# Logsumexp over heads on one core: new sharing of the heads between engines in the last fifteen tiles, and 1 MB half tiles for the last seven instead of two

## The chip, the cores and the metric

The kernel runs on one core of a Trainium2 chip. The metric is the device time in microseconds (us) of one execution. The profile's span, from the first to the last instruction, is about 2 us shorter than that time (335.9 us for 338.01 in the profiled run of the kernel before, 332.8 for 334.57 after the change). Five kinds of engine do the work in these kernels: PE (matrix products), ACT (one function on each element), DVE (products and sums of vectors), POOL (here mainly the adds of the bias) and the DMA engines, which move data; the SP queue issues the loads and most of the output. The tiles lie in SBUF; PE writes to PSUM, a second memory from which ACT and DVE read here (L165 and L193 of the kernel before).

## The reference

```
x: (8, 2048, 2048) f32, bias: (8, 256) f32       # 8 heads of 256 columns
x_heads = x.reshape(B, S, H, Dh).transpose(0, 2, 1, 3) + bias[None, :, None, :]
x_tiled = np.repeat(x_heads, 2, axis=2)          # each row twice
out     = max + log(sum(exp(x_tiled - max)))     # over the 256 columns of a head
```

So 134 MB are read once, and for every row and head one number is written twice. Inputs are random normal, so the kernels leave the maximum out. The sum needs either exp(x + b), or exp(x) times the weight exp(b).

## The kernel before

The input is cut into 64 tiles of 2 MB (128 partitions x 2 rows x 2048 columns), nine of them in SBUF at once. In a tile the eight heads are treated in three ways:

- PE heads (2): PE adds the bias while it copies the columns to PSUM (a 3-row matmul of the bias, then a matmul by the identity); ACT takes the exponential and sums it in one instruction for each head and row.
- POOL heads (4): POOL adds the bias in SBUF, ACT takes the exponential, DVE sums.
- DVE heads (2): ACT takes the exponential without the bias, DVE multiplies by the weights exp(b) and sums.

The steady part does tile t's adds, then the exponentials and sums of tile t - 1. "Bulk" below means this.

```
def exp_and_sum(t):                              # for tile t, called one tile later
    v = xts[t % NBUF][:, :, CPE:D]               # 6 heads: 4 with POOL's bias, 2 without
    exp_inplace(v)                               # ACT, L202
    f = v[:, :, CG:CW]
    nc.vector.tensor_tensor(out=f, in0=f, in1=w_tile, op=ALU.mult)     # DVE, L193
    nc.vector.tensor_reduce(out=R[b][:, :, NPE:H, blk], ...)           # DVE, L194
...
for t in range(T):
    if left >= NLATE:                            # all but the last two tiles
        got = add_bias([xt[:, k, 0:CPE] for k in range(K)])            # PE, L154, L159
        g_add(t)                                                       # POOL, L186
    if 0 < t and left >= NLATE - 1:
        exp_and_sum(t - 1)
    if left >= NLATE:
        for k in range(K): sum_biased(got[k], ...)                     # ACT, L165
    for k0, k1, c0, c1 in pieces(t) if left < NLATE else []:           # last two tiles
        ...  exp_inplace(...); sum_biased(...)
        weigh(...)       # DVE, L208: multiply by the weights and sum, one head and row each
    if 0 < t and t - 1 + NBUF < T: load(t - 1 + NBUF)                  # SP queue
```

The last two tiles (62 and 63) are "prompt": no POOL, each piece done as it comes, six heads by DVE's weighted sums. They are loaded as halves (1 MB, one of the two rows) and, at the very end, smaller pieces. At the end of each batch of 8 tiles, `finish` transposes the sums on PE (L224), takes the logarithm on ACT (L237), and sends it out by DMA.

The softmax here doesn't subtract the row's maximum and nothing guards it: scores larger than these inputs give would overflow.

## Time and profile before

| | before |
|---|---|
| time, median of 4 runs | 337.78 us (337.74 to 337.91) |
| span of the profiled run | 335.9 us |
| landing of a 2 MB tile | every 4.9 us |
| last piece of input landed (landing records of the trace) | 322.1 us |

These are lines of the page of the kernel before: busy us of each engine with its share of the span, then busy tenths in 40 slices of 8.4 us, the busy share of the DMA engines and the GB/s.

```profile
span 335.9 us, 2193 instructions
PE 236.6 (70%) x410; PEld 69.5 (21%) x410; DVE 290.2 (86%) x174; ACT 296.1 (88%) x598; POOL 291.6 (87%) x84
...
DVE  0019999999999999989989999988999999979995
ACT  1379999899999999999899999998999889899994
DMA  7999999999999999999999999999999999999900
GB/s 296 430 427 435 429 424 427 433 423 427 428 425 430 433 423 430 425 428 431 424 433 421 429 427 425 434 432 423 425 430 427 433 427 426 427 429 418 386 23 16
```

The DMA row is full from the second slice to the 38th: the loads bound the run until about 322 us. From the second slice to the 36th the rate is 421 to 435 GB/s; whether the loads themselves could be made faster was not tested. Three engines are at 86 to 88%, yet none of them sets the pace there: on the page POOL waits 23.8 us in all for loaded tiles, ACT 9.8 us for POOL, and DVE 34.1 us for ACT (22.7 of them before its first tile). In the last two slices the DMA is idle and ACT and DVE still work: that is the part that can be shortened. The next lines are groups of instructions, from the page: line, engine, operation, tiles, shapes and count, then busy us and the mean ns of one, then idle time just before.

```profile
L186 POOL TENSOR_TENSOR xt<-xt,b_rep 128x2048 f32<-128x2048 f32 x62 | 281.2, 4537 | 26.2 <-DMA xt<-in_x_dram 23.8
L194 DVE TENSOR_REDUCE R<-xt 128x12 f32<-128x3072 f32 x62 | 208.0, 3355 | 7.2 <-DVE xt L193 1.0
L193 DVE TENSOR_TENSOR xt<-xt,w_rep 128x1024 f32<-128x1024 f32 x62 | 75.5, 1218 | 34.3 <-ACT xt L202 34.1
L208 DVE CUSTOM_DVE_ANT_0 junk<-xt,w_rep 128x256 f32<-128x256 f32 x24 | 8.3, 416 | 0.0
```

A bulk tile goes through POOL (4.54 us), ACT (2.76 us) and DVE (1.22 + 3.36 us) one after the other. Each fits into 4.9 us, but one tile needs the sum of them. The timeline of the kernel before shows what this means at the end (start us, duration us, engine, line, operation; in brackets the idle time before it and what ended it):

```profile
312.17 4.54 POOL L186 TENSOR_TENSOR xt<-xt,b_rep 128x2048 f32<-128x2048 f32 x1 [0.35 <-DMA xt<-in_x_dram]
...
316.74 4.14 ACT L202 ACTIVATE xt<-xt 128x3072 f32<-128x3072 f32 x2 [0.34 <-POOL xt L186]
...
319.54 1.22 DVE L193 TENSOR_TENSOR xt<-xt,w_rep 128x1024 f32<-128x1024 f32 x1 [0.22 <-ACT xt L202]
324.13 0.41 DVE L208 CUSTOM_DVE_ANT_0 junk<-xt,w_rep 128x256 f32<-128x256 f32 x1
```

Tile 61, the last bulk tile, landed at 312.0 and left DVE at 324.2, 12.2 us later. Only then could DVE begin with the prompt sums of tile 62, although its first half had landed at 314.5. From the chain of work that ended last in the kernel before (start us, duration us, what):

```profile
327.97 0.33 DVE junk L208
...
332.07 0.33 DVE junk L208
332.46 0.39 PE tpair L224
332.88 0.37 ACT res L237
```

The run ends with a row of DVE's weighted sums, 24 in all at one every 0.342 us (324.13 to 332.41), then a transpose, a logarithm and 2.6 us of output.

### The profile page before, as it was taken

How to read it: one execution, taken by the hardware profiler on the slowest of the kernel's cores; microseconds unless marked ns; L12 is line 12 of the kernel's file. 1: busy time of each engine (PE TensorE's matmuls, PEld its weight loads, DVE VectorE, ACT ScalarE, POOL GpSimd, SP SyncE). 2: the span in 40 equal slices, each digit the busy share in tenths (PEclk: the TensorE clock that was granted, in tenths of full speed). 3: DMA queues.
4: the chain of work that ended last, by engine and by line, in shares of the span. 5: the costliest groups of instructions: out<-in, count | busy, mean ns of one | idle time of the engine just before them, and what ended most of it. 6: DMA issues, size and time to landing. Idle time of an engine off the chain costs nothing. (4 is left out here: it accounts for less than half of the span.)

```text
span 335.9 us, 2193 instructions
## 1 busy us (share of the span) xinstructions
PE 236.6 (70%) x410; PEld 69.5 (21%) x410; DVE 290.2 (86%) x174; ACT 296.1 (88%) x598; POOL 291.6 (87%) x84
## 2 busy tenths in 40 slices
PE   5297687796766866677577669867668695767761
PEld 2022221222121221122122112212112221212110
DVE  0019999999999999989989999988999999979995
ACT  1379999899999999999899999998999889899994
POOL 6999989979989999899898999898998999889613
PEclk9998965559789589876987775676987659587875
DMA  7999999999999999999999999999999999999900
GB/s 296 430 427 435 429 424 427 433 423 427 428 425 430 433 423 430 425 428 431 424 433 421 429 427 425 434 432 423 425 430 427 433 427 426 427 429 418 386 23 16
DMA packets 11199, 135.41 MB, mean 403 GB/s; under 512 B 1577, under 2 KB 1849, under 8 KB 2993
## 3 DMA queue, kind: packets, MB, share of 16 engines
q1 hardware_dynamic: 10832, 135.17, 95.1%
q0 software_dynamic: 352, 0.10, 0.2%
q8 instruction: 3, 0.05, 0.1%
q14 instruction: 10, 0.08, 0.1%
q10 hardware_dynamic: 2, 0.01, 0.0%
HBM read 134.23 MB, written 1.05 MB: 403 GB/s over the span
## 5 line engine op out<-in xcount | busy, mean ns | idle before, releaser
L186 POOL TENSOR_TENSOR xt<-xt,b_rep 128x2048 f32<-128x2048 f32 x62 | 281.2, 4537 | 26.2 <-DMA xt<-in_x_dram 23.8
L159 PE MATMUL ps<-xt,ident 128*128 128x512 f32 x256 | 183.5, 855 | 66.2 <-DMA xt<-in_x_dram 65.7
L194 DVE TENSOR_REDUCE R<-xt 128x12 f32<-128x3072 f32 x62 | 208.0, 3355 | 7.2 <-DVE xt L193 1.0
L202 ACT ACTIVATE xt<-xt 128x3072 f32<-128x3072 f32 (+3 forms) x70 | 177.5, 2539 | 10.2 <-POOL xt L186 9.8
L165 ACT ACTIVATE ps<-ps 128x256 f32<-128x256 f32 x256 | 94.6, 369 | 17.2 <-PE ps L159 12.7
L193 DVE TENSOR_TENSOR xt<-xt,w_rep 128x1024 f32<-128x1024 f32 x62 | 75.5, 1218 | 34.3 <-ACT xt L202 34.1
L159 PEld LDWEIGHTS ps<-xt,ident 128*128 128x128 f32 x256 | 57.5, 249 | 153.9 <-DMA xt<-in_x_dram 98.5
L154 PE MATMUL ps<-b,ones 3*128 3x512 bf16 x128 | 48.0, 450 | 12.6 <-DMA b<-bparts 6.5
L165 ACT ACTIVATION_READ_ACCUMULATOR ps<-ps 128x1 f32 x256 | 48.8, 191 | 0.0
L154 PEld LDWEIGHTS <-ones 3*128 3x128 bf16 x128 | 7.8, 97 | 78.2 <-issue 78.2
L258 POOL DMA_DIRECT2D out_dram<-res x8 | 4.0, 508 | 9.5 <-ACT res L237 9.5
L224 PE MATMUL tpair<-ident,R 128*64 128x128 f32 (+1 forms) x16 | 4.3, 367 | 10.0 <-DVE R L194 10.0
L208 DVE CUSTOM_DVE_ANT_0 junk<-xt,w_rep 128x256 f32<-128x256 f32 x24 | 8.3, 416 | 0.0
L132 PE MATMUL w_rep<-brow,ones 1*128 1x512 f32 x6 | 5.5, 1078 | 3.4 <-DMA brow<-in_bias_dram 3.4
L237 ACT ACTIVATE res<-tpair 64x512 f32<-64x512 f32 (+3 forms) x11 | 6.0, 543 | 2.0 <-PE tpair L224 2.0
L139 ACT ACTIVATE b_rep<-w_rep 128x1024 f32<-128x1024 f32 x1 | 1.0, 1025 | 6.9 <-PE w_rep L132 6.9
L224 PEld LDWEIGHTS tpair<-ident,R 128*64 128x64 f32 (+1 forms) x16 | 1.9, 143 | 19.2 <-DVE R L194 16.4
L224 PE MATMUL tpair<-ident,Rz 128*8 128x128 f32 x2 | 0.7, 372 | 3.4 <-ACT xt L202 1.8
L132 PEld LDWEIGHTS w_rep<-brow,ones 1*128 1x128 f32 x6 | 1.8, 325 | 5.4 <-issue 5.4
L121 POOL CAST bparts<-brow 1x512 bf16<-1x512 f32 x1 | 0.6, 601 | 2.0 <-DMA brow<-in_bias_dram 2.0
L105 ACT ACT_TABLE_LOAD x1 | 1.3, 1283 | 0.7 <-PEq L344 0.7
L142 ACT ACTIVATE w_rep<-w_rep 128x512 f32<-128x512 f32 x3 | 1.7, 582 | 0.1
(18 smaller groups left out, 9.5 us busy)
## 6 DMA issues: line engine op xcount, KB each, us to landing
xt<-in_x_dram SPq DMA_DIRECT2D x62, 2048.0 KB, 32.0
xt<-in_x_dram SPq DMA_DIRECT2D x2, 1024.0 KB, 30.0
xt<-in_x_dram SPq DMA_DIRECT2D x2, 512.0 KB
out_dram<-res SPq DMA_DIRECT2D x7, 128.0 KB, 30.1
xt<-in_x_dram SPq DMA_DIRECT2D x3, 256.0 KB, 16.4
xt<-in_x_dram SPq DMA_DIRECT2D x2, 128.0 KB, 8.7
out_dram<-res POOLq DMA_DIRECT2D x8, 12.0 KB, 1.7
b<-bparts POOLq DMA_DIRECT2D x3, 1.0 KB, 5.7
```

What stands on the lines that cost most here:

```text
L132: nc.tensor.matmul(w_rep[:, c : c + MM], lhsT=ones, rhs=brow[:, CPE + c : CPE + c + MM], start=True, stop=True,)
L154: nc.tensor.matmul(p[:, 0:CPE], lhsT=ones3, rhs=b3, start=True, stop=False)
L159: nc.tensor.matmul(p[:, 0:CPE], lhsT=ident, rhs=v, start=False, stop=True)
L165: nc.scalar.activation(out=p[:, c : c + Dh], in_=p[:, c : c + Dh], func=ACT.Exp, accum_out=dst(h),)
L186: nc.gpsimd.tensor_tensor(out=v, in0=v, in1=b_tile, op=ALU.add)
L193: nc.vector.tensor_tensor(out=f, in0=f, in1=w_tile, op=ALU.mult)
L194: nc.vector.tensor_reduce(out=R[b][:, :, NPE:H, blk], in_=v.rearrange("p k (h j) -> p k h j", j=Dh), op=ALU.add, axis=mybir.AxisListType.X,)
L202: nc.scalar.activation(out=v, in_=v, func=ACT.Exp)
L208: nc.vector.tensor_tensor_reduce(out=j, in0=v, in1=w_rep[:, c : c + Dh], scale=1.0, scalar=0.0, op0=ALU.mult, op1=ALU.add, accum_out=dst,)
L224: nc.tensor.transpose(out=tps[i][0:nr, k], in_=src(k), identity=ident)
L237: nc.scalar.activation(out=rv, in_=tv, func=ACT.Ln)
L258: engine.dma_start(out=ov, in_=iv)
```

## The change

The intent is to have less work left when the last data land. Tiles 0 to 48 stay bulk (other columns go to each engine, the amounts are the same). From tile 49 a "mixed" stage: PE takes one head, POOL three, and DVE weighs the other four at once, without waiting for POOL. From tile 57 tiles are loaded and worked on as two halves. From tile 61 all is prompt. Weights used beside POOL's adds are in PSUM (`w_ps`); those of the heads that only the prompt stage weighs are in SBUF (`w_sb`).

```
-NPE = 2
-CG = 1024
-NLATE = 2
+BULK = dict(pe=2, g0=4, late=True)      # pe: PE heads; g0: first POOL head; late: DVE heads wait
+MIXED = dict(pe=1, g0=5, late=False)
+PROMPT = dict(pe=2, g0=8, late=False)
+STAGES = [(0, BULK, False), (49, MIXED, False), (57, MIXED, True), (61, PROMPT, True)]
-LAST_CUTS = [[0, 1024, 2048], [0, 512, 1024, 1536, 1792, 2048]]
+LAST_CUTS = [[0, 2048], [0, 1024, 1536, 2048]]
... (ps: five buffers for four; w_ps, w_sb; add_bias, g_add and exp_and_sum take a stage and rows)
+        for k0, k1, c0, c1 in pieces(t):
+            if c0 == 0:
+                got = add_bias(m, ...)                          # PE
+                if with_pool: g_add(m, xt, k0, k1)              # POOL
+            if waiting: waiting()        # the piece before: exponential and sums of its POOL heads
+            if h0 < h1 and not m["late"]: exp_inplace(...)      # ACT, at once
+            if c0 == 0: ... sum_biased(m, ...)                  # ACT
+            if not m["late"]: ... weigh(...)                    # DVE, at once
+            waiting = next_waiting                              # also issues the load of tile t + 9
```

More of the change, by code (lines that the diff above doesn't have):

```diff
@@ L43 @@
     T = B * NBLK
-    CPE = NPE * Dh
-    CW = D - CPE
+    CPE = 2 * Dh
     MM = 512
-    assert CPE <= MM
+    W0, G0, W1 = Dh, 4 * Dh, 5 * Dh
     sb = ctx.enter_context(tc.tile_pool(name="sb", bufs=1))
@@ L54 @@
     brow = sb.tile([1, D], F32, name="brow")
-    b_rep = sb.tile([P, CG], F32, name="b_rep")
+    b_rep = sb.tile([P, D - G0], F32, name="b_rep")
+    w_sb = sb.tile([P, D - W1], F32, name="w_sb")
     ident = sb.tile([P, P], F32, name="ident")
@@ L69, with mode_of, halves_of @@
     xts = [sb.tile([P, K, D], F32, name=f"xt{i}") for i in range(NBUF)]
-    w_rep = pp.tile([P, CW], F32, name="w_rep")
-    ps = [pp.tile([P, MM], F32, name=f"ps{i}") for i in range(4)]
+    w_ps = pp.tile([P, W1 - W0], F32, name="w_ps")
+    ps = [pp.tile([P, MM], F32, name=f"ps{i}") for i in range(5)]
     tpair = pp.tile([P, 2, K, P], F32, name="tpair")
     tps = [tpair[:, i] for i in range(2)]
+    def mode_of(t):
+        return [m for t0, m, _ in STAGES if t0 <= t][-1]
+    def halves_of(t):
+        return [s for t0, _, s in STAGES if t0 <= t][-1]
     def pieces(t):
-        left = T - 1 - t
-        if left > 1:
+        if not halves_of(t):
             return [(0, K, 0, D)]
-        cuts = [[0, D]] * K if left else LAST_CUTS
+        cuts = [[0, D]] * K if t < T - 1 else LAST_CUTS
         return [
@@ L127, with spread, add_bias @@
         nc.gpsimd.dma_start(out=b3[i : i + 1, :], in_=bparts[:, i])
-    for c in range(0, CW, MM):
+    def spread(dst, c0, c1):
         nc.tensor.matmul(
-            w_rep[:, c : c + MM],
-            lhsT=ones,
-            rhs=brow[:, CPE + c : CPE + c + MM],
-            start=True,
-            stop=True,
-        )
-    nc.scalar.activation(out=b_rep, in_=w_rep[:, 0 : CG], func=ACT.Copy)
-    for c in range(0, CW, MM):
-        w = w_rep[:, c : c + MM]
+            dst, lhsT=ones, rhs=brow[:, c0:c1], start=True, stop=True
+        )
+    for i, c in enumerate(range(G0, D, MM)):
+        spread(ps[i], c, c + MM)
+        nc.scalar.activation(
+            out=b_rep[:, c - G0 : c - G0 + MM], in_=ps[i], func=ACT.Copy
+        )
+    for c in range(W0, W1, MM):
+        w = w_ps[:, c - W0 : c - W0 + MM]
+        spread(w, c, c + MM)
         nc.scalar.activation(out=w, in_=w, func=ACT.Exp)
+    nc.scalar.activation(out=w_sb, in_=b_rep[:, W1 - G0 :], func=ACT.Exp)
     n_ps = [0]
     n_junk = [0]
-    def add_bias(views):
+    def add_bias(m, views):
+        n = m["pe"] * Dh
         got = []
@@ L154, in add_bias @@
             nc.tensor.matmul(
-                p[:, 0:CPE], lhsT=ones3, rhs=b3, start=True, stop=False
+                p[:, 0:n], lhsT=ones3, rhs=b3[:, 0:n], start=True, stop=False
             )
@@ L158, in add_bias, with sum_biased @@
         for p, v in zip(got, views):
-            nc.tensor.matmul(p[:, 0:CPE], lhsT=ident, rhs=v, start=False, stop=True)
+            nc.tensor.matmul(p[:, 0:n], lhsT=ident, rhs=v, start=False, stop=True)
         return got
-    def sum_biased(p, dst):
-        for h in range(NPE):
+    def sum_biased(m, p, dst):
+        for h in range(m["pe"]):
             c = h * Dh
@@ L170, in sum_biased, with each_row, g_add, exp_inplace @@
             )
-    b_tile = bass.AP(
-        tensor=b_rep.tensor,
-        offset=b_rep.offset,
-        ap=[b_rep.ap[0], [0, K], [1, CG]],
-    )
-    w_tile = bass.AP(
-        tensor=w_rep.tensor,
-        offset=w_rep.offset + CG,
-        ap=[w_rep.ap[0], [0, K], [1, CW - CG]],
-    )
-    def g_add(t):
-        v = xts[t % NBUF][:, :, CPE : CPE + CG]
-        nc.gpsimd.tensor_tensor(out=v, in0=v, in1=b_tile, op=ALU.add)
-    def exp_and_sum(t):
-        b, blk = divmod(t, NBLK)
-        v = xts[t % NBUF][:, :, CPE:D]
-        exp_inplace(v)
-        f = v[:, :, CG:CW]
-        nc.vector.tensor_tensor(out=f, in0=f, in1=w_tile, op=ALU.mult)
+    def each_row(src, c, n, k_rows):
+        return bass.AP(
+            tensor=src.tensor,
+            offset=src.offset + c,
+            ap=[src.ap[0], [0, k_rows], [1, n]],
+        )
+    def g_add(m, xt, k0, k1):
+        c = m["g0"] * Dh
+        v = xt[:, k0:k1, c:D]
+        nc.gpsimd.tensor_tensor(
+            out=v, in0=v, in1=each_row(b_rep, c - G0, D - c, k1 - k0), op=ALU.add
+        )
+    def exp_inplace(v):
+        nc.scalar.activation(out=v, in_=v, func=ACT.Exp)
+    def later(m, xt, k0, k1, sums):
+        h0 = m["pe"] if m["late"] else m["g0"]
+        v = xt[:, k0:k1, h0 * Dh : D]
+        exp_inplace(v)
+        if m["late"]:
+            n = (m["g0"] - h0) * Dh
+            f = v[:, :, 0:n]
+            nc.vector.tensor_tensor(
+                out=f,
+                in0=f,
+                in1=each_row(w_ps, h0 * Dh - W0, n, k1 - k0),
+                op=ALU.mult,
+            )
         nc.vector.tensor_reduce(
-            out=R[b][:, :, NPE:H, blk],
+            out=sums[:, k0:k1, h0:H],
             in_=v.rearrange("p k (h j) -> p k h j", j=Dh),
@@ L199, in exp_and_sum @@
         )
-    def exp_inplace(v):
-        nc.scalar.activation(out=v, in_=v, func=ACT.Exp)
     def weigh(v, h, dst):
-        c = h * Dh - CPE
+        c = h * Dh
+        w = w_ps[:, c - W0 : c - W0 + Dh] if c < W1 else w_sb[:, c - W1 : c - W1 + Dh]
         j = junk[n_junk[0] % 2]
@@ L210, in weigh @@
             in0=v,
-            in1=w_rep[:, c : c + Dh],
+            in1=w,
             scale=1.0,
@@ L272, in finish_batch, with sums_of @@
         )
+    def sums_of(t):
+        b, blk = divmod(t, NBLK)
+        if t < T - 2:
+            return R[b][:, :, :, blk]
+        return Ry if t < T - 1 else Rz
+    waiting = None
     for t in range(T):
-        b, blk = divmod(t, NBLK)
+        m = mode_of(t)
         xt = xts[t % NBUF]
-        left = T - 1 - t
-        def sum_at(k, h):
-            if left > 1:
-                return R[b][:, k, h, blk : blk + 1]
-            return (Ry if left else Rz)[:, k, h : h + 1]
-        if left >= NLATE:
-            got = add_bias([xt[:, k, 0:CPE] for k in range(K)])
-            g_add(t)
-        if 0 < t and left >= NLATE - 1:
-            exp_and_sum(t - 1)
-        if left >= NLATE:
-            for k in range(K):
-                sum_biased(got[k], lambda h: sum_at(k, h))
-        for k0, k1, c0, c1 in pieces(t) if left < NLATE else []:
-            if left == 0 and c1 == D and k0 > 0:
+        sums = sums_of(t)
+        with_pool = m["g0"] < H
+        for k0, k1, c0, c1 in pieces(t):
+            if t == T - 1 and c1 == D and k0 > 0:
                 finish(
@@ L305, with next_waiting @@
             if c0 == 0:
-                got = add_bias([xt[:, k, 0:CPE] for k in range(k0, k1)])
-            w0 = max(c0, CPE)
-            if w0 < c1:
-                exp_inplace(xt[:, k0:k1, w0:c1])
+                got = add_bias(m, [xt[:, k, 0 : m["pe"] * Dh] for k in range(k0, k1)])
+                if with_pool:
+                    g_add(m, xt, k0, k1)
+            if waiting:
+                waiting()
+            h0 = max(c0 // Dh, m["pe"])
+            h1 = min(c1 // Dh, m["g0"])
+            if h0 < h1 and not m["late"]:
+                exp_inplace(xt[:, k0:k1, h0 * Dh : h1 * Dh])
             if c0 == 0:
                 for k in range(k0, k1):
-                    sum_biased(got[k - k0], lambda h: sum_at(k, h))
-            for k in range(k0, k1):
-                for c in range(w0, c1, Dh):
-                    weigh(xt[:, k, c : c + Dh], c // Dh, sum_at(k, c // Dh))
-            if left == 0 and c0 == 0:
+                    sum_biased(m, got[k - k0], lambda h: sums[:, k, h : h + 1])
+            if not m["late"]:
+                for k in range(k0, k1):
+                    for h in range(h0, h1):
+                        weigh(
+                            xt[:, k, h * Dh : (h + 1) * Dh], h, sums[:, k, h : h + 1]
+                        )
+            def next_waiting(t=t, m=m, xt=xt, k0=k0, k1=k1, sums=sums):
+                if m["g0"] < H:
+                    later(m, xt, k0, k1, sums)
+                if k1 == K and t + NBUF < T:
+                    load(t + NBUF)
+            waiting = next_waiting
+            if t == T - 1 and c0 == 0:
                 if k0 == 0:
@@ L320 @@
                     finish(B - 1, lambda k: Ry[:, k], 1, K, S - 2 * K * P, 0, nc.sync)
-        if 0 < t and t - 1 + NBUF < T:
-            load(t - 1 + NBUF)
         fb, at = divmod(t - 2, NBLK)
```

## The prediction

> **What bounds the kernel now.** The loads. The page's slices show the DMA at 9 tenths and about 428 GB/s from slice 2 to slice 36; the waits show PE (65.7 us) and POOL (23.8 us) waiting for loaded tiles; 2 MB land every 4.9 us. POOL's add (4.54 us), DVE (1.22 + 3.35 us) and ACT (about 4.8 us) fit inside that. What can shorten is the end: the last piece lands at about 322.4 us of the 335.9 us span, leaving 13.4 us behind the loads. In the timeline ACT starts tile 61's bulk exponential only at 316.7, 4.7 us after that tile landed, because POOL's add comes first; tile 62's first prompt exponential is then done at about 324, although that half landed at 314.5. Then DVE's 24 weighted sums, 0.342 us each, run without a gap from 324.1 to 332.4 (the chain that ended last is this row), then a transpose, a logarithm and an output DMA (2.6 us).
>
> **What the change does.** Tiles 0 to 48: same work, other heads to each engine. Tiles 49 to 60: POOL keeps 3 heads (estimate scaled from the trace: 3.4 us a tile), DVE weighs 4 heads at once and reduces 3 (4.5 us a tile, as before), ACT about 4.3 us. Tiles 61 to 63: no POOL; per 1 MB half DVE does 6 x 0.342 = 2.05 us and ACT 1.4 + 0.9 = 2.3 us, against 2.45 to 2.5 us between halves. So each half should be done 1 to 3 us after landing, and the 24-sum backlog should be gone.
>
> **Cost.** 8 KB packets took 39.1 ns per KB against 38.3 for 16 KB (packet records of the trace), so 10 MB more of them cost 0.3 to 0.5 us; fewer small pieces in the last tile give about that back. Loads end at 322.4 again, +-0.4.
>
> **What is left at the end.** The first half of tile 63 lands near 319.8; then on ACT in order: exponential, two sums, logarithm of batch 7, exponential of 512 columns, two sums (behind PE's 2 us matmul at the low clock seen in the last slices), logarithm of tile 62, two more 512-column exponentials: finished between 326.2 (PE at full clock) and 328.2 (half clock). Then two weighted sums, transpose, logarithm, output: 4.3 us. Span 330.5 to 332.4. The time is 2 us above the span, as before: 333.5 us, a gain of 4.3 us or 1.3%. Range 331.8 to 335.6.
>
> [...]
>
> **What would show it.** Tile period 4.9 us up to tile 56; last landing 322 to 323; no row of 24 sums on DVE in the last 9 us; bulk exponentials gone after tile 60; the chain at the end shared by ACT, PE and DVE; ACT ending 4 to 6 us after the last landing.
>
> **What would make it wrong.** A half's matmul (2.0 us plus 0.5 us for the bias at the low clock) overrunning 2.45 us, so PE backlogs; DVE's sums slowed beside POOL; half-tile loads slower, or starved, as each new load waits for an older one to land.
>
> Faster by over 2%: 0.09; within 2%: 0.90; slower: 0.01.

## The result, and the profile after

| | before | after |
|---|---|---|
| time, median of 4 runs | 337.78 us | 334.73 us (334.41 to 335.22) |
| ratio, 95% interval | | 0.991 (0.9893 to 0.9927) |
| last input landed | 322.1 us | 322.3 us |
| first half of tile 62: landed, left DVE | 314.5, 326.2 us | 314.6, 318.7 us |
| last weighted sum ended | 332.4 us | 329.4 us |
| span | 335.9 us | 332.8 us |

A ratio is the mean time of one kernel's fast runs over that of the other's of the same rounds, so it is not quite the ratio of the medians. The change is 0.9% faster; at a threshold of 2% that counts as the same. The loads end where they ended; the 3 us come from behind them.

The same lines of the page, after:

```profile
span 332.8 us, 2370 instructions
...
DVE  0019999999999999999999899999899999999982
ACT  2269999899999999989989999998999988899983
DMA  7999999999999999999999999999999999999940
GB/s 298 428 433 431 423 432 429 427 425 427 426 432 426 427 431 426 425 432 427 426 429 425 431 427 427 427 430 427 431 426 428 425 429 424 418 420 420 422 155 17
```

DVE is nearly empty in the last slice. With half tiles the rate is 418 to 422 GB/s for 427 before them; a half lands every 2.49 us. The next view is the busy time by stretch (us busy and instructions of each engine; granted clock, which is the share of full speed that the trace shows PE to have been given; DMA share; GB/s), first for the kernel before:

```profile
250.00:280.00 30.00, 23.00 (x38) 6.57 (x38) 27.86 (x13) 27.58 (x57) 27.54 (x7) 0.72 1.01 429
324.00:336.00 12.00, 4.50 (x9) 1.14 (x9) 8.41 (x49) 6.78 (x19) 4.00 (x8) 0.51 0.05 12
```

The columns after the length are PE, PE's weight loads, DVE, ACT and POOL. The kernel after:

```profile
250.00:280.00 30.00, 15.76 (x38) 7.58 (x38) 29.64 (x89) 27.18 (x43) 22.15 (x7) 0.54 1.01 428
280.00:300.00 20.00, 11.85 (x26) 5.56 (x27) 20.00 (x79) 18.19 (x30) 14.39 (x8) 0.50 1.01 420
324.00:333.00 9.00, 1.36 (x5) 0.25 (x3) 2.23 (x12) 3.21 (x9) 3.64 (x8) 0.69 0.07 16
```

After 324 us DVE has 2.2 us of work left instead of 8.4. In the mixed stage POOL has less to do (22 us of 30 for 27.5), DVE is busy all the time, and PE has less to do; its granted clock is 0.54 in the first of these stretches and 0.50 in the second. e12 below asks whether the one comes from the other. The timeline of ACT in the kernel after, at the end (the 0.2 us reads of ACT's accumulator between are left out):

```profile
321.89 0.37 ACT L177 ACTIVATE ps<-ps 128x256 f32<-128x256 f32 x1 [0.31 <-PE ps L171]
...
324.53 0.37 ACT L177 ACTIVATE ps<-ps 128x256 f32<-128x256 f32 x1 [0.66 <-PE ps L171]
...
325.41 0.57 ACT L257 ACTIVATE res<-tpair 8x512 f32<-8x512 f32 x1
325.89 0.61 ACT L200 ACTIVATE xt<-xt 128x512 f32<-128x512 f32 x1
327.68 0.37 ACT L257 ACTIVATE res<-tpair 8x256 f32<-8x256 f32 x1 [1.17 <-DMA out_dram<-res]
327.96 0.61 ACT L200 ACTIVATE xt<-xt 128x512 f32<-128x512 f32 x1
329.94 0.37 ACT L257 ACTIVATE res<-tpair 8x256 f32<-8x256 f32 x1 [1.37 <-PE tpair L244]
```

And the end of its chain of work that ended last:

```profile
325.52 0.48 ACT res L257
326.01 1.58 DMA out_dram<-res
...
327.96 0.62 ACT xt L200
328.60 0.43 DVE junk L228
...
329.53 0.39 PE tpair L244
329.94 0.37 ACT res L257
```

The row of DVE's sums is gone from the chain. In its place stand PE, ACT, and a DMA that nobody had in mind: the logarithm at 327.68 writes the first half's results into a buffer whose former contents (tile 62's results) an output DMA is still reading. In this trace ACT takes its work in the order of the program: the exponential of the very last piece, which landed at 322.3, waits behind that logarithm until 327.96.

### The profile page after: what moved, and what is told of

Its sections match the earlier page's. It is cut to its first block, busy times and chain, and to the rows that moved or that the text cites. A ratio compares the mean times of both kernels' runs of the same rounds, so it can differ in the third digit from the quotient of the medians.

```text
span 332.8 us, 2370 instructions
## 1 busy us (share of the span) xinstructions
PE 227.3 (68%) x412; PEld 72.1 (22%) x412; DVE 288.3 (87%) x380; ACT 292.2 (88%) x570; POOL 274.8 (83%) x87
## 4 chain that ended last, share of the span: by engine, by line
DMA 63%; ACT 10%; issue 8%; POOL 7%; PE 6%; DVE 4%; DVEq 0%; POOLq 0%; SPq 0%; ACTq 0%
DMA xt<-in_x_dram 60%; ACT xt L200 7%; POOL xt L195 5%; PE ps L171 4%; DVE xt L210 3%; ACT ps L177 2%; DMA b<-bparts 2%; DVE R L216 1%; PE ps L166 1%; DMA brow<-in_bias_dram 1%; DMA out_dram<-res 0%; PE tpair L244 0%; POOL brest L133 0%; POOL brest L131 0%; ACT res L257 0%
## 5 line engine op out<-in xcount | busy, mean ns | idle before, releaser
L195 POOL TENSOR_TENSOR xt<-xt,b_rep 128x2048 f32<-128x2048 f32 (+2 forms) x65 | 264.5, 4071 | 35.1 <-DMA xt<-in_x_dram 29.1
L171 PE MATMUL ps<-xt,ident 128*128 128x512 f32 (+1 forms) x256 | 174.2, 817 | 74.9 <-DMA xt<-in_x_dram 74.5
L200 ACT ACTIVATE xt<-xt 128x3072 f32<-128x3072 f32 (+3 forms) x89 | 184.9, 2096 | 12.3 <-POOL xt L195 11.6
L216 DVE TENSOR_REDUCE R<-xt 128x12 f32<-128x3072 f32 (+2 forms) x65 | 185.9, 2860 | 5.8 <-DVE xt L210 1.0
L177 ACT ACTIVATE ps<-ps 128x256 f32<-128x256 f32 x232 | 85.7, 369 | 14.3 <-PE ps L171 10.5
L210 DVE TENSOR_TENSOR xt<-xt,w_ps 128x1024 f32<-128x1024 f32 x49 | 59.6, 1217 | 30.0 <-ACT xt L200 30.0
L166 PE MATMUL ps<-b,ones 3*128 3x512 bf16 (+1 forms) x128 | 46.9, 437 | 8.7 <-ACT ps L177 4.8
L228 DVE CUSTOM_DVE_ANT_0 junk<-xt,w_ps 128x256 f32<-128x256 f32 x114 | 40.5, 412 | 3.1 <-ACT xt L200 2.7
L228 DVE DVE_READ_ACCUMULATOR2_ANT R<- 128x1 f32 x108 | 8.5, 79 | 0.0
L228 DVE CUSTOM_DVE_ANT_0 junk<-xt,w_sb 128x256 f32<-128x256 f32 x18 | 6.8, 421 | 1.3 <-ACT xt L200 1.3
```

The costliest lines, as they stand in the source:

```text
L166: nc.tensor.matmul(p[:, 0:n], lhsT=ones3, rhs=b3[:, 0:n], start=True, stop=False)
L171: nc.tensor.matmul(p[:, 0:n], lhsT=ident, rhs=v, start=False, stop=True)
L177: nc.scalar.activation(out=p[:, c : c + Dh], in_=p[:, c : c + Dh], func=ACT.Exp, accum_out=dst(h),)
L195: nc.gpsimd.tensor_tensor(out=v, in0=v, in1=each_row(b_rep, c - G0, D - c, k1 - k0), op=ALU.add)
L200: nc.scalar.activation(out=v, in_=v, func=ACT.Exp)
L210: nc.vector.tensor_tensor(out=f, in0=f, in1=each_row(w_ps, h0 * Dh - W0, n, k1 - k0), op=ALU.mult,)
```

## The experiments

Twelve kernels ran (there is none with the label e11), in three groups; all gave correct results. Runs of one group share the runs of the kernel before (medians 337.81, 337.91 and 337.83 us). Unless said otherwise each is an edit of the changed kernel. Theory A is that of the prediction: what counts is the work that DVE and ACT still have when the last data land, and both the new sharing and the half tiles reduce it. Its rivals are named in the expectations.

| run | time, us | ratio to before, 95% interval |
|---|---|---|
| the change | 334.73 | 0.991 (0.9893 to 0.9927) |
| e1 old stages, new cuts | 338.03 | 1.0004 (0.9991 to 1.0016) |
| e2 new sharing, whole tiles to 61 | 334.18 | 0.989 (0.9877 to 0.9904) |
| e3 half tiles, bulk sharing | 337.7 | 0.9995 (0.9982 to 1.0007) |
| e4 prompt from 61 only | 336.75 | 0.9963 (0.9949 to 0.9976) |
| e5 own result buffers | 333.84 | 0.9868 (0.9848 to 0.9888) |
| e6 e5, logarithms last | 332.25 | 0.9828 (0.9814 to 0.9843) |
| e7 e6, mixed tiles whole | 333.03 | 0.9852 (0.9838 to 0.9867) |
| e8 e2, mixed stage 57 to 60 | 334.7 | 0.9902 (0.9885 to 0.9918) |
| e9 all weights in SBUF | 357.63 | 1.0585 (1.057 to 1.0599) |
| e10 prompt from 55, no mixed stage | 334.85 | 0.991 (0.9896 to 0.9923) |
| e12 PE kept busy in the mixed stage | 334.87 | 0.9899 (0.9883 to 0.9916) |
| e13 e6, one logarithm for tile 63 | 332.5 | 0.9839 (0.9825 to 0.9852) |

### Which part of the change is it? (e1 to e4)

**e1_none** leaves only the new cuts and columns:

```
-STAGES = [(0, BULK, False), (49, MIXED, False), (57, MIXED, True), (61, PROMPT, True)]
+STAGES = [(0, BULK, False), (62, PROMPT, True)]
```

> The changed kernel with the old stages: bulk sharing up to tile 61, prompt from 62, half tiles from 62 only; the new cuts of the last tile and the new head columns stay. Theory A (the gain comes from the backlog behind the last landing that the stages remove): no gain, 337.3 to 338.3 us, and DVE again ends with a row of about 24 weighted sums without gaps. Rival C (the gain comes from the coarser cuts of the last tile or the other columns): 335 us or less.

It took 338.03 us, as expected: the cuts and the columns by themselves give nothing of the gain. DVE again ran without a gap, from 319.4 to 331.6 us.

**e2_mixed_whole** keeps the sharing and drops the half tiles before tile 62:

```
+STAGES = [(0, BULK, False), (49, MIXED, False), (61, PROMPT, False), (62, PROMPT, True)]
```

> Head sharing changes as in the change (mixed from 49, prompt from 61), but tiles up to 61 are loaded and worked on as whole 2 MB tiles. Theory A (both parts drain the backlog, the sharing is the larger): tile 61 starts 2.4 us later, so 335.0 to 336.2 us, most of the gain of 3 us kept less about 1 us. Rival B (half tiles do it): 337 us or more.

334.18 us: the whole gain, more than I expected. **e3_halves_bulk** does the opposite, half tiles with the bulk sharing:

```
+STAGES = [(0, BULK, False), (57, BULK, True), (62, PROMPT, True)]
```

> Half tiles from 57 as in the change, but with the bulk sharing of heads up to tile 61; no mixed stage. My sum of the durations says each engine still fits into a half (POOL 2.3, DVE 2.4, ACT 2.3 us of 2.48), so the wait on POOL's add halves: about 335.0 to 336.0 us. Rival B (half tiles do it) says 334.5 to 335.0, the same as the change. If the sharing does it: 337 or more.

337.7 us: no gain, and my expectation fell by 2 us. DVE's timeline in this run shows why:

```profile
294.57 1.22 DVE L210 TENSOR_TENSOR xt<-xt,w_ps 128x1024 f32<-128x1024 f32 x1 [0.88 <-ACT xt L200]
295.90 3.35 DVE L216 TENSOR_REDUCE R<-xt 128x12 f32<-128x3072 f32 x1
299.17 0.68 DVE L210 TENSOR_TENSOR xt<-xt,w_ps 128x512 f32<-128x512 f32 x1
299.95 1.76 DVE L216 TENSOR_REDUCE R<-xt 128x6 f32<-128x1536 f32 x1
301.62 0.68 DVE L210 TENSOR_TENSOR xt<-xt,w_ps 128x512 f32<-128x512 f32 x1
302.40 1.75 DVE L216 TENSOR_REDUCE R<-xt 128x6 f32<-128x1536 f32 x1
```

Smaller pieces should be done sooner, and POOL and ACT do finish them sooner (2.37 us for POOL's add of a half and 4.54 of a whole tile, 1.47 and 2.76 us for ACT's exponential). But DVE was occupied with the last whole tile until 299.2, and from then on it takes 2.45 us for each half (299.17 to 301.62) while a half lands every 2.48 us. It sheds 0.03 us of its lateness per half, about 0.4 us in the ten halves, and has no gap from 294.6 until 331.3 us. Halving the tile doubles the number of instructions: two halves cost it 4.9 us, a whole tile 4.60 us (294.57 to 299.17, from start to start as for the halves). The lateness that the pipeline of whole tiles had is handed on as a backlog.

**e4_prompt61** starts the prompt stage one tile earlier and has no mixed stage:

```
+STAGES = [(0, BULK, False), (61, PROMPT, True)]
```

> Only one more tile prompt and in halves (61 instead of 62 on), everything before as bulk. Theory A: tile 60's bulk work still ends at about 319 on DVE, then 36 sums of 0.342 us follow, about 331.5: 336.5 to 337.3 us, a gain of about 1 us. Rival D (the stage that matters is the prompt one alone, because POOL is out of tile 61): 334.5 to 335.0, the whole gain.

336.75 us, as theory A has it: a third of the gain, with DVE without a gap over 0.2 us from 314.5 to 331.9.

### Is it the mixed stage, or any sharing that gives DVE less work? (e8, e10)

**e8_short_mixed** has four mixed tiles instead of twelve:

```
+STAGES = [(0, BULK, False), (57, MIXED, False), (61, PROMPT, False), (62, PROMPT, True)]
```

> The kernel of mixed whole tiles (334.18 us) with the mixed stage over tiles 57 to 60 only instead of 49 to 60. Theory A (DVE carries a backlog of about 12 us out of the bulk stage and mixed tiles drain it by only 0.4 us each, 4.5 us of work per 4.9 us): DVE is still behind at tile 61 and ends in a row without gaps, 334.9 to 335.7 us. Rival F (the gain comes at once, from the last few tiles not waiting for POOL): 334.0 to 334.5.

334.7 us, between the two ranges. The picture is that of theory A: DVE has no gap from 294.6 to 328.5 us, and in the trace a mixed tile takes it 4.40 us (299.22 to 303.62), so 0.5 us of lateness goes per tile. The time is better than expected. In the profile the end of the run then waits for ACT and for the output DMA (1.39 us before ACT's logarithm) as in the changed kernel, and the last backlog of DVE hides behind that. So four mixed tiles keep 3.2 us of the 3.6 us that e2 gains with twelve, with that wait in place.

**e10_prompt_only** has no mixed stage, but seven more prompt tiles:

```
+STAGES = [(0, BULK, False), (55, PROMPT, False), (61, PROMPT, False), (62, PROMPT, True)]
```

> No mixed stage: bulk to tile 54, then prompt whole tiles (PE 2 heads, DVE 6 heads, POOL nothing) from 55, halves from 62. Theory A (what counts is that DVE's work per tile is under the 4.9 us between landings early enough; prompt needs 12 x 0.342 = 4.1 us, ACT 4.6 us): the backlog of about 7 us drains in 7 tiles, 333.8 to 334.9 us, the same as the mixed stage. Rival (POOL's share is needed to keep pace in those tiles): 335.5 us or more.

334.85 us, within noise of the changed kernel. Prompt tiles take DVE 4.1 us; it had caught up at 309.6, where its first gap is. POOL's share is not needed in these tiles. What e2, e8, e10 and the change have in common is DVE work of 4.1 to 4.5 us for a tile that lands every 4.9 us, begun some tiles before the end.

They have a second thing in common: DVE's weighted sums do not wait for POOL. In the bulk stage a tile is 4.60 us of work for DVE (e3), so there would be 0.3 us of slack in it; but DVE spends most of this waiting for ACT's exponential, which comes after POOL's add (0.22 us before 319.54 in the timeline of the kernel before). A mixed tile leaves 0.5 us by the work alone (4.4 us), only 0.2 us more; what is new besides is that DVE has sums that it may begin before POOL is done. e3 shows that work which comes sooner gives nothing without slack. No run has the slack of the mixed stage with DVE still waiting for POOL, so the shares of the two are not separated.

### What sets the end of the changed kernel? (e5, e6, e7, e13, e12)

**e5_own_res** takes away the wait for the output DMA by other buffers:

```
-    res = [... for i in range(2)]
+    res = [... for i in range(4)]        # tile 63: first half res[2], second half res[3]
```

> The changed kernel with two more result buffers, so that the logarithms of the last tile's two halves no longer write a buffer that an output DMA is still reading. Theory A (this wait of 1.17 us before the last exponential lies on the chain): 333.4 to 333.8 us, 1.0 to 1.2 us less than the changed kernel, and no wait of ACT for an output DMA. Rival: ACT would otherwise wait for PE or DVE there, then under 0.4 us less.

333.84 us (332.55 to 334.0), 0.9 us less than the change by the medians of two groups, a little short of what I expected. The profiled run no longer waits for the DMA, but its waits for PE in the same place were 0.52 and 0.99 us, longer than in the profile of the change (0.31 and 0.66); so the wait was on the chain, and part of its removal was taken by another. These two waits were short in some runs and long in others for a reason that was not found (e12).

**e6_logs_last** changes ACT's order for the last half: three exponentials, two sums, three logarithms. (The result buffers are again chosen so that none is waited for.)

```
-            if c0 == 0:                                          # sums at the first piece
+            last_half = t == T - 1 and k0 == K - 1
+            if c1 == D if last_half else c0 == 0:                # last half: at its last piece
                 for k in range(k0, k1): sum_biased(...)
-    (finish of tile 62 after the first piece, of tile 63's first half before the last piece)
+    finish(B - 1, lambda k: Ry[:, k], 1, K, S - 2 * K * P, 0, nc.sync)
+    finish(B - 1, lambda _: Rz[:, 0], 1, 1, S - 2 * P, 3, nc.sync)
     finish(B - 1, lambda _: Rz[:, K - 1], 1, 1, S - P, 2, nc.sync)
```

> As the run before, and on ACT the three exponentials of the last half come first, then the two sums, then the last three logarithms. Theory A (the last exponential is late because logarithms and sums stand ahead of it in ACT's order, the sums waiting for PE's matmul at the low clock): last exponential ends near 324.9 instead of 328.6, end bounded by the sums, 331.4 to 332.2 us. Rival E (the end is set by PE or DVE whatever ACT's order): 333.2 us or more.

332.25 us (332.02 to 332.3), close to the range, and faster than e5 in the same group. ACT's timeline in this run:

```profile
323.06 1.66 ACT L200 ACTIVATE xt<-xt 128x512 f32<-128x512 f32 x3
324.62 0.37 ACT L177 ACTIVATE ps<-ps 128x256 f32<-128x256 f32 x1
...
325.52 0.57 ACT L257 ACTIVATE res<-tpair 8x512 f32<-8x512 f32 x1
326.55 0.37 ACT L257 ACTIVATE res<-tpair 8x256 f32<-8x256 f32 x1 [0.47 <-PE tpair L244]
327.39 0.37 ACT L257 ACTIVATE res<-tpair 8x256 f32<-8x256 f32 x1 [0.47 <-PE tpair L244]
```

The last exponential ends at 324.7 instead of 328.6, and PE's matmul is ready before the sums come. This is the fastest kernel, 1.7% under the kernel before.

**e7_best** is e6 with the mixed tiles 57 to 60 whole again:

```
+STAGES = [(0, BULK, False), (49, MIXED, False), (61, PROMPT, True)]
```

> As the run before, with the mixed tiles 57 to 60 whole (2 MB) and half tiles from 61 on. Since half tiles in the mixed stage gained nothing and cost some 0.3 us of load time: 331.2 to 332.0 us, at or a little under the run before. If half tiles in the mixed stage help once the end is cleaned up: 332.3 us or more.

333.03 us, 0.8 us slower than e6 in the same group: here the half tiles do help. The profiles suggest why. In both kernels tile 61 is in halves; with tile 60 whole, ACT waits for POOL's add of a whole mixed tile (0.82 us idle before 310.77) and starts the prompt exponentials later: the one of tile 63's first half ends at 322.7 instead of 321.8, and no slack is left to catch up. With the waits at the end that the changed kernel has, this difference did not show (e2 was even a little faster than the change).

**e13_one_log** joins the last two logarithms of e6 and their outputs:

```
-    finish(B - 1, lambda _: Rz[:, 0], 1, 1, S - 2 * P, 3, nc.sync)
-    finish(B - 1, lambda _: Rz[:, K - 1], 1, 1, S - P, 2, nc.sync)
+    finish(B - 1, lambda k: Rz[:, k], 1, K, S - 2 * P, 3, nc.sync, k_major=True)
```

> The kernel with the logarithms last (332.25 us), with one logarithm and one output DMA for both halves of the last tile. The last three logarithms there waited for PE's transposes in turn (0.47 us each); one of them and one wait go: 331.7 to 332.1 us. If the longer logarithm and transfer eat it: 332.2 us or more.

332.5 us: no gain. The last logarithm ended at 327.2 instead of 327.8, but from there to the end of the span it took 3.1 us (327.2 to 330.3), against 2.4 us in e6 (327.8 to 330.2). The one output has 16 KB where the last of the two had 8 KB; whether its size alone makes these 0.7 us was not tested.

**e12_pe_fed** asks whether the low PE clock matters. In the changed kernel the granted clock is one half from 252 to 314 us and again from 317 to 324, and ACT waits for PE at the end.

```
+            for _ in range(2 if m["pe"] == 1 else 0):      # overwritten by the next matmul
+                nc.tensor.matmul(p, lhsT=ones3, rhs=b3, start=True, stop=True)
             nc.tensor.matmul(p[:, 0:n], lhsT=ones3, rhs=b3[:, 0:n], start=True, stop=False)
```

> The changed kernel with two more bias matmuls for each head group in the mixed stage, overwritten by the real one, so that PE stays as busy as in the bulk stage. Theory G (the granted clock stayed at half from 252 us on because PE had half the work in the mixed stage, and ACT's waits for PE near the end, 0.3 and 0.66 us, come from that): the clock alternates again in the mixed stage and the time is 333.7 to 334.4 us. Rival: the clock at the end is not set by the mixed stage, 334.5 to 335.3 us.

334.87 us (333.66 to 335.32): no gain in the median. The lever did not work, as a stretch of this run shows:

```profile
250.00:280.00 30.00, 28.23 (x68) 12.15 (x67) 29.63 (x89) 27.41 (x45) 22.14 (x7) 0.50 1.01 427
```

PE was busy 94% of these 30 us (77% in the kernel before, at a mean clock of 0.72), and the clock still stayed at one half, from 243 to 321.5 us. So theory G is wrong as I stated it: busy time of these small matmuls did not raise the clock. (The profile models when a matmul ends, so its busy share may be too high.) What a full clock at the end would be worth was not tested, since no edit brought it about. Among the five runs, the two quickest (333.66 and 333.83) and the other three (334.87 to 335.32) differ by about 1.2 us. The profile is of one of the two; in it the clock was full from 321.5 to 328 us and ACT did not wait for PE at the end. In the profile of the change the clock was half from 317.2 to 324.0 and ACT waited 0.97 us there. That the spread of these kernels comes from where this window falls is likely, but not shown: the runs without a profile have only a mean clock.

### Why weights in PSUM? (e9)

**e9_sbuf_weights** has DVE read all its weights for the weighted sums from SBUF:

```
-    w_sb = sb.tile([P, D - W1], F32, name="w_sb")
+    w_sb = sb.tile([P, D - W0], F32, name="w_sb")          # heads 1 to 7 instead of 5 to 7
-        w = w_ps[...] if c < W1 else w_sb[...]
+        w = w_sb[:, c - W0 : c - W0 + Dh]
```

> The changed kernel with all weights of the weighted sums in SBUF, so that in the mixed stage DVE reads two SBUF inputs while POOL adds. If the two exclude each other[...]: a mixed half needs 1.82 (POOL) + 4 x 0.342 (sums) = 3.2 us against 2.48 between landings, so the stage falls behind by up to 10 us: 338 to 346 us, with POOL's add or DVE's sums visibly longer in it. If they do not: 334.4 to 335.2, as the changed kernel.

357.63 us, 23 us slower than the change: DVE's weighted sums are held while POOL adds (one for 3.65 us), and that cost more than I allowed for. Two of its groups, and in the timeline one of POOL's adds with the DVE sums around it:

```profile
L229 DVE CUSTOM_DVE_ANT_0 junk<-xt,w_sb 128x256 f32<-128x256 f32 x132 | 74.0, 619 | 0.3 <-ACT xt L201 0.3
L196 POOL TENSOR_TENSOR xt<-xt,b_rep 128x1536 f32<-128x1536 f32 x8 | 27.8, 3472 | 10.6 <-DMA xt<-in_x_dram 6.3 <-DVE R L229 4.3
...
271.65 0.41 DVE L229 CUSTOM_DVE_ANT_0 junk<-xt,w_sb 128x256 f32<-128x256 f32 x1
271.87 3.49 POOL L196 TENSOR_TENSOR xt<-xt,b_rep 128x1536 f32<-128x1536 f32 x1 [1.47 <-DVE R L229]
272.00 3.65 DVE L229 CUSTOM_DVE_ANT_0 junk<-xt,w_sb 128x256 f32<-128x256 f32 x1
275.58 0.41 DVE L229 CUSTOM_DVE_ANT_0 junk<-xt,w_sb 128x256 f32<-128x256 f32 x1
```

A sum takes 0.41 us beside an idle POOL. One that starts while POOL's add is running ends only some 0.3 us after that add: 275.65 after 275.36 here, so that it takes 3.65 us; 1.9 to 2.6 us where it starts in the middle of such an add, and 2.0 us with the add of a half. Thirteen sums were held like this, and DVE's sums took 74.0 us in all, for 47.3 us (40.5 + 6.8) in the change; that is about the loss. POOL's adds are hardly longer: 3.47 us for a whole tile (3.45 in the change) and 1.91 us for a half (1.82). With the weights in PSUM the change shows 0.412 us for each of 114 sums, 96 of which are in the mixed stage.

## Why the prediction was right or wrong

The time (334.73 us for 333.5, range 331.8 to 335.6): right.

- **Bound by the loads, gain only at the end: right.** The loads end at 322.3 us after and 322.1 before. The 322.4 in the prediction was the landing of a small output DMA queued behind the loads; the last input came 0.3 us earlier. That made no difference.
- **The row of 24 sums goes: right.** 8.4 us of DVE work after 324 us became 2.2 us. e1 and e4 show that it is this backlog.
- **Each half done 1 to 3 us after landing: too low.** ACT was done after 2.7 us (tile 62's first half: 314.6 to 317.3), DVE after 4.1 us (318.7). DVE's sums start when ACT's exponential is done; by the prediction's own durations the two in turn need 1.4 + 2.05 us, more than its 3 us.
- **Which part does it: not separated in the prediction, and my expectation in e3 was wrong.** The sharing of heads gives the gain (e2), the half tiles alone give none (e3), since a half of bulk work keeps DVE busy 2.45 us of 2.48.
- **Last exponential at 326.2 to 328.2 us: it ended at 328.6.** The prediction's list of ACT's work leaves out one instruction, the logarithm of the first half of tile 63, which the kernel puts before the very last exponential. It cost 1.17 us of waiting for a result buffer that an output DMA was reading, and 0.28 us of its own (327.68 to 327.96). Without these 1.45 us the exponential would have ended at 327.1, in the middle of the range. So the path was right and one term of its sum was missing; it is about as large as the whole difference between the predicted and the measured time (1.2 us). e5 took 0.9 us off by giving the logarithm a buffer.
- **The waits for PE: smaller than allowed for.** They came as foreseen (0.31 and 0.66 us), with the clock at one half from 317.2 to 324.0 us but not after; for the half clock the prediction had 328.2 us, and without the missing term it would have been 327.1. That this error and the missing term have opposite signs is luck.
- **The rest after the last exponential: 4.3 us predicted, 4.2 measured** (328.6 to 332.8).
- **Half tiles load slower by 0.3 to 0.5 us: right in size** (2.49 us each for 2.45). Starvation did not come: the DMA share was 1.01 from 280 to 300 us.
- **DVE's sums slowed beside POOL: named as a risk, and it did not come.** With the weights in PSUM a sum takes 0.412 us in the change (0.416 in the kernel before, whose sums run after POOL's last add). e9, with them in SBUF, shows what was at stake: up to 3.65 us for a sum, and 357.63 us in all.

## What to carry to other kernels

When loads set the pace, look at how late each engine is when the last data land, not only at how busy it is: an engine that hands over late catches up only by the slack in each tile (here 0.03 us per half tile in the bulk sharing, 0.5 us per tile in the mixed one), so the lighter sharing must begin early enough before the end, and smaller pieces alone may give nothing. After a backlog is gone, follow the chain again: here a result buffer still read by an output DMA and the order of ACT's work were worth 2.5 us together (e6), nearly as much as the change itself. And check small buffers at the end of a kernel as carefully as the large ones in its loop.
